# Column sums in four column groups, and a first stage in written order

## The chip, the cores and the metric

The kernel runs on one core of a Trainium2 chip, as a single launch. The metric is the device time of an execution in microseconds (us). The median of three runs before the change is 720.83 us (720.08 to 723.85).

PE is TensorE (matrix products into PSUM; PEld is its weight load), DVE is VectorE, ACT is ScalarE, POOL is GpSimd, and SP is the engine whose queue issues nearly all transfers.

## The reference, cut to what matters

One decoder block in fp32 with a sequence of 256 tokens, a model width D of 1024, and one conditioning row `c`:

```python
mod = silu(c) @ w_ada + b_ada                 # 1024 x 6144
sh1, sc1, g1, sh2, sc2, g2 = split(mod, 6)
h = rmsnorm(x, norm1_g) * (1 + sc1) + sh1
proj = h @ w_in                               # 1024 x 5120
# MoBA attention and differential attention from parts of proj,
# merged by sigmoid gates, projected by w_out
x = x + g1 * (merged @ w_out)
h2 = rmsnorm(x, norm2_g) * (1 + sc2) + sh2
x = x + g2 * moe(h2)                          # 32 experts, top 2 of one group
out = rmsnorm(x, final_g)
```

The change concerns `c @ w_ada` (the modulation, a product with a single row), the first `rmsnorm`, and the first products with `w_in`. The experts' weights, read later, are most of the bytes moved.

## The kernel before, in words

The stage that the change touches goes as follows. `x` is held as two tiles of 128 tokens. Each is squared and summed, the inverse root is taken by POOL's power (`rstd`, L335), the tile is scaled into `xn`, and sixteen transposes (L460) bring it into `xT`, with D on the partitions. `c` is transposed into `ccol` (L451), eight columns of 128.

For each quarter `q` of D (256 rows of `w_in`, so two chunks of 128) the modulation's `sc1` and `sh1` are needed for 256 columns. `ada_first(q)` (L376) makes them. In the first quarter both column blocks, later only `sh1`, are summed on PE (L387): the column `ccol[:, k]`, spread over 32 columns, is the stationary operand, and the product lands in partitions 32*(k % 4) and the 31 after it, so that four values of k share the array as four column groups. The block is evicted by ACT (L388). In the later quarters `sc1` is summed by DVE in eight operations (`ada_part`, L368 and L370). `ada_first_sum(q)` (L391) then turns the sums into columns with four small products (L397), which also add the four groups up, and three DVE operations (L399 to L401) make `modT`. `make_h` (L469) forms h (DVE, L471), its rounded part `xH` (ACT, L473) and the remainder `xL` (DVE, L474). `split` (L479) does the same to a weight chunk: ACT rounds it (L483), and DVE or POOL, in turn, subtracts (L486). `piece` (L489) then runs three products for each chunk and token tile (L496, L497, L498): `xH` by the rounded weights, `xL` by the rounded weights, `xH` by the remainder. In each of the four passes this is done for three blocks of 512 columns: k (into `acck`), q (`accq`) and v (`accv`). On PE the pass is written so:

```python
        piece(acck, chunks[0], xH, xL, 2 * q, q == 3)
        if q < 3:
            ada_first(q + 1)
        piece(accq, chunks[1], xH, xL, 2 * q, q == 3)
        if q < 3:
            ada_first_sum(q + 1)
            make_h(2 * q + 2)
        piece(accv, chunks[2], xH, xL, 2 * q, q == 3)
```

After the four passes come four small transposes (`p6`, L553), and the rest of the block follows. Between its further products stand eight units of the modulation: `ada_four(u)` (L403) sums 512 columns on PE (L409, again with four values of k as four column groups), ACT evicts them (L413), and `ada_sum(u)` (L415) turns them with four products (L430). In units 6 to 9 the columns of one product are taken with a step of four, in units 10 and 11 as whole blocks. Units 4 and 5 are turned in another way (L423).

Two things set the order of the work. Transfers are issued by SP in a list written out by hand (`order`), each as soon as its buffer is free. On the other engines the framework's scheduler orders the instructions, except inside `tc.manual_schedule(engines=...)`, where those engines keep the order of the program's text. SP is so ordered throughout, and from the first norm to `p6` so is PE (L447), but neither ACT nor DVE nor POOL.

Of the kernel before, what the change touches and what calls it, by code (L numbers as in the profile page):

```python
# [116 lines left out]
def tile_block(ctx: ExitStack, tc: tile.TileContext, d, out):  # L117
# [186 lines left out]

    io128 = cp.tile([128, 128], F32, name="io128")
# [3 lines left out]
    ident = cp.tile([128, 128], F32, name="ident")  # L309
    ve.tensor_scalar(ident, io128, pix, None, op0=OP.is_equal)  # L310
# [3 lines left out]
    ve.memset(nhalf, -0.5)  # L314
    th = cp.tile([128, 1], F32, name="th")
# [30 lines left out]
    gb1 = cp.tile([128, 2, KC], F32, name="gb1")  # L346
# [8 lines left out]
    def scale_base(i, g, b):  # L355
        ve.scalar_tensor_tensor(gb1[:, i, :], b, 1.0, g, op0=OP.add, op1=OP.mult)

# [5 lines left out]
    def ada_part(part, w, k0):  # L363

        for j in range(w.shape[1]):
            k = k0 + j
            if k == 0:
                ve.tensor_scalar(part, w[:, j, :], ccol[:, k:k + 1], None, op0=OP.mult)  # L368
            else:
                ve.scalar_tensor_tensor(part, w[:, j, :], ccol[:, k:k + 1], part, op0=OP.mult, op1=OP.add)  # L370

# [3 lines left out]

    def ada_first(q):  # L376

        p = wk(f"adc{q}")
        part = parts["first"] = turns["part"].new([2, 256])
        for i, n in enumerate((1, 0)):  # L380
            w = got[("adc", n, q)]
            o = p[:, 256 * i:256 * i + 256]
            if q and i == 0:
                ada_part(part[:, 0, :], w, 0)
            else:
                for k in range(KC):
                    te.matmul(o[32 * (k % 4):32 * (k % 4) + 32, :], c32(k), w[:, k, :], start=k < 4, stop=k >= 4)  # L387
                sc.activation(part[:, i, :], o, AF.Copy)  # L388
            done(("adc", n, q))

    def ada_first_sum(q):  # L391

        part, r = parts["first"], wk(f"adq{q}")
        k = slice(2 * q, 2 * q + 2)
        for i in range(2):
            for j in range(2):
                te.matmul(r[:, 2 * i + j:2 * i + j + 1], part[:, i, 128 * j:128 * j + 128],  # L397
                          ones[:, 0:1] if q and i == 0 else th, start=True, stop=True)
        ve.tensor_tensor(modT[:, 0, k], r[:, 0:2], vec[:, R_N1 + 2 * q:R_N1 + 2 * q + 2], op=OP.mult)  # L399
        ve.tensor_tensor(modT[:, 0, k], modT[:, 0, k], gb1[:, 0, k], op=OP.add)  # L400
        ve.tensor_tensor(modT[:, 1, k], r[:, 2:4], vec[:, R_B + 2 * q:R_B + 2 * q + 2], op=OP.add)  # L401

    def ada_four(u):  # L403

        p = wk(f"ada{u}")
        for h in range(2):
# [5 lines left out]
        parts[u] = turns["part"].new([512])  # L412
        sc.activation(parts[u], p, AF.Copy)  # L413

    def ada_sum(u):  # L415

        part = parts.pop(u)
        if u in (4, 5):
            q = wk(f"adaq{u}")
# [7 lines left out]
        q = wk(f"adaq{u}")  # L427
        for i in range(4):
            cols = slice(i, 512, 4) if seg in (3, 4) else slice(128 * i, 128 * i + 128)
            te.matmul(q[:, i:i + 1], part[:, cols], th, start=True, stop=True)  # L430
        if seg == 4:
            ve.tensor_tensor(modT[:, 2, k], q[:, 0:4], vecp[:, 0, k], op=OP.mult)
            ve.tensor_tensor(modT[:, 2, k], modT[:, 2, k], gb1[:, 1, k], op=OP.add)
# [12 lines left out]
    manual = ExitStack()  # L446
    manual.enter_context(tc.manual_schedule(engines={mybir.EngineType.PE}))  # L447
    ss1 = cp.tile([128, 2], F32, name="ss1")
    wps = wk("warm")
    warm(12, wps)  # L450
    sc.activation(ccol, columns(crow, KC, "crow"), AF.Silu)  # L451
    for t in range(2):
        ve.scalar_tensor_tensor(xn[:, t, :], x_sb[:, t, :], 1.0, x_sb[:, t, :], op0=OP.mult, op1=OP.mult,
                                accum_out=ss1[:, t:t + 1])
        rs1 = rstd(ss1[:, t:t + 1], D, f"rs1{t}")
        ve.tensor_scalar(xn[:, t, :], x_sb[:, t, :], rs1, None, op0=OP.mult)
# [9 lines left out]
    ve.tensor_copy(vec, columns(vrow, R_N, "vec_ps"))  # L466
    scale_base(0, vec[:, R_N1:R_N1 + 8], vec[:, R_B + 8:R_B + 16])

    def make_h(k0):  # L469
        for k in range(k0, k0 + 2):  # L470
            ve.tensor_scalar(hT[:, k, :], xT[:, k, :], modT[:, 0, k:k + 1], modT[:, 1, k:k + 1],  # L471
                             op0=OP.mult, op1=OP.add)
            sc.activation(xH[:, k, :], hT[:, k, :], AF.Copy)  # L473
            ve.tensor_sub(xL[:, k, :], hT[:, k, :], xH[:, k, :].bitcast(F32))  # L474
# [4 lines left out]
    def split(w, k0, n, name):  # L479
# [5 lines left out]
        nsplit[0] += 1  # L485
# [3 lines left out]
    def piece(acc, chunk, lh, ll, k0, last, ts=(0, 1)):  # L489
# [3 lines left out]
        for k in range(n):  # L493
# [36 lines left out]


    ada_first(0)
    ada_first_sum(0)
    acck, accq, accv = accs("ink"), accs("inq"), [wk(f"inv{t}") for t in range(2)]
    warm(4, acck[0])
    make_h(0)
    upto(("winq", 2, 3))
    for q in range(4):
        chunks = [split(got[("winq", u, q)], 0, 2, f"wq{u}{q}") for u in (1, 0, 2)]
        for u in (1, 0, 2):  # L540
# [9 lines left out]
        piece(accv, chunks[2], xH, xL, 2 * q, q == 3)  # L550
# [5 lines left out]
    scale_base(1, vecp[:, 0, :], vecp[:, 1, :])  # L556
# [714 lines left out]
```

## Time and profile before

| | |
|---|---|
| median of three runs | 720.83 us (720.08 to 723.85) |
| the profiled execution's own time | 719.79 us |
| its span, first to last instruction | 718.0 us |
| mean granted TensorE clock | 0.934 of full speed |
| busy: PE / DVE / ACT / POOL | 79% / 39% / 21% / 12% of the span |
| moved by DMA | 259.09 MB, 361 GB/s over the span |

The busy shares are means over stages that differ, so a stage has to be read by itself. A share of DMA of about 1 means that the transfer engines are busy all the time. A matmul's duration includes the way through the array, so that consecutive ones overlap: their pace is read from the chain of waits, which counts each only from the end of the one before.

### The profile page before, as it was taken

Reading aid. Unit: us, or ns where it says so; the run is one execution under the profiler, and the core shown is the slowest. Engines: PE = TensorE matmul, PEld = TensorE weight load, DVE = VectorE, ACT = ScalarE, POOL = GpSimd, SP = SyncE. Lnnn points to the kernel's source line nnn. Section 1 sums busy time; section 2 is a strip of 40 time slices with the busy share of each in tenths; the row PEclk is TensorE's granted clock in tenths of the full one; section 3 lists DMA queues with packets and bytes.
Section 4 is the critical chain, followed back from the end, with each engine's and each line's share of the span. In section 5 each row is a group of like instructions: output and inputs, shape, how many; then the busy total and the mean of one; then the engine's idle time right before and its main releaser. Section 6 shows DMA issues by size and latency. Waiting matters only on the chain.

```text
span 718.0 us, 11923 instructions
## 1 busy us (share of the span) xinstructions
PE 567.4 (79%) x4909; PEld 372.3 (52%) x4909; DVE 282.2 (39%) x806; ACT 147.8 (21%) x330; POOL 86.2 (12%) x73
## 2 busy tenths in 40 slices
PE   7989999999999998898886855965866685587374
PEld 3667666656777765564643522622623453264232
DVE  5778744545126647543432321321312121132105
ACT  2325664556444512000000000000000000000002
POOL 2225213315334310000000000000000000000001
PEclk9999999999999999899998988998998898899888
DMA  9999938909885798999999999999999999999992
GB/s 315 366 377 387 382 113 312 344 7 363 319 336 207 267 361 287 328 428 422 421 421 422 428 421 421 423 424 425 422 419 423 424 424 424 421 422 424 419 390 93
DMA packets 63582, 259.09 MB, mean 361 GB/s; under 512 B 6223, under 2 KB 16672, under 8 KB 45094
## 3 DMA queue, kind: packets, MB, share of 16 engines
q1 hardware_dynamic: 63430, 258.27, 91.4%
q8 instruction: 40, 0.66, 0.4%
q14 instruction: 16, 0.13, 0.0%
q10 hardware_dynamic: 96, 0.03, 0.0%
HBM read 257.23 MB, written 1.05 MB: 360 GB/s over the span
## 4 chain that ended last, share of the span: by engine, by line
DMA 51%; PE 33%; DVE 8%; issue 3%; ACT 2%; SPq 1%; POOL 1%; POOLq 0%; DVEq 0%; ACTq 0%
DMA gu<-in_w_up_dram 23%; DMA gu<-in_w_gate_dram 17%; DMA dn<-in_w_down_dram 10%; PE gu L979 3%; PE in L497 3%; PE in L496 3%; PE in L498 3%; PE xe L905 2%; PE dn L983 2%; PE ada L409 2%; DMA winq<-in_w_in_dram 1%; DVE part L370 1%; PE wo L496 1%; PE wo L497 1%; PE wo L498 1%
## 5 line engine op out<-in xcount | busy, mean ns | idle before, releaser
L979 PE MATMUL gu<-gu,xe 128*32 128x256 f32 x2048 | 137.4, 420 | 58.6 <-DMA gu<-in_w_up_dram 52.4
L979 PEld LDWEIGHTS gu<-gu,xe 128*32 128x32 f32 x2048 | 73.3, 118 | 117.5 <-issue 82.2
L983 PE MATMUL dn<-dn,hq 128*32 128x256 f32 x992 | 72.0, 439 | 59.2 <-DMA dn<-in_w_down_dram 42.2
L989 DVE TENSOR_TENSOR dq<-dn,g2g 32x256 f32<-32x256 f32 x124 | 52.1, 420 | 96.0 <-PE dn L983 92.5
L983 PEld LDWEIGHTS dn<-dn,hq 128*32 128x32 f32 x992 | 37.3, 123 | 93.3 <-issue 48.6
L970 ACT ACTIVATE hid<-gu 128x128 f32<-128x128 f32 x32 | 8.9, 278 | 347.1 <-PE gu L979 336.6
L971 DVE TENSOR_TENSOR hid<-hid,gu 128x128 f32<-128x128 f32 x32 | 9.2, 288 | 172.0 <-ACT hid L970 172.0
L905 PEld LDWEIGHTS xe<-pr,x 128*128 128x128 f32 x256 | 60.3, 329 | 4.2 <-issue 4.2
L905 PE MATMUL xe<-pr,x 128*128 128x128 f32 (+1 forms) x256 | 61.9, 403 | 0.0
L1074 POOL TENSOR_TENSOR fo<-fo,tail 128x512 f32<-128x512 f32 x2 | 2.5, 1272 | 442.3 <-ACT tail L1072 442.3
L486 POOL TENSOR_TENSOR win<-win,win 128x512 fp32r<-128x512 f32 x28 | 38.8, 1388 | 86.3 <-ACT win L483 79.4
L496 PE MATMUL in<-win,xH 128*128 128x512 f32 x112 | 45.7, 408 | 0.0
L497 PE MATMUL in<-win,xL 128*128 128x512 f32 x112 | 45.6, 407 | 0.0
L498 PE MATMUL in<-win,xH 128*128 128x512 f32 x112 | 45.2, 403 | 0.0
L483 ACT ACTIVATE win<-win 128x512 fp32r<-128x512 f32 x56 | 34.5, 629 | 20.4 <-PE in L498 19.7
L909 DVE TENSOR_SCALAR xe<-xe,modT 128x128 f32<-128x128 f32 (+1 forms) x64 | 21.6, 402 | 35.1 <-PE xe L905 35.1
L955 PE MATMUL y<-dq,pt 128*128 128x512 f32 x56 | 26.2, 610 | 5.9 <-DVE dq L989 5.8
L486 DVE TENSOR_TENSOR win<-win,win 128x512 fp32r<-128x512 f32 x28 | 22.7, 812 | 19.9 <-ACT win L483 17.8
L496 PEld LDWEIGHTS in<-win,xH 128*128 128x128 f32 x112 | 21.1, 188 | 7.8 <-issue 2.3
L497 PEld LDWEIGHTS in<-win,xL 128*128 128x128 f32 x112 | 21.2, 189 | 6.9 <-issue 3.2
L498 PEld LDWEIGHTS in<-win,xH 128*128 128x128 f32 x112 | 21.1, 188 | 6.7 <-issue 2.9
L955 PEld LDWEIGHTS y<-dq,pt 128*128 128x128 f32 x56 | 9.5, 189 | 20.2 <-DVE dq L989 13.5
(344 smaller groups left out, 755.2 us busy)
## 6 DMA issues: line engine op xcount, KB each, us to landing
gu<-in_w_gate_dram SPq DMA_DIRECT2D x54, 1024.0 KB, 22.9
gu<-in_w_up_dram SPq DMA_DIRECT2D x54, 1024.0 KB, 22.7
dn<-in_w_down_dram SPq DMA_DIRECT2D x26, 2048.0 KB, 24.7
ada<-in_w_ada_dram SPq DMA_DIRECT2D x16, 1024.0 KB, 10.8
win<-in_w_in_dram SPq DMA_DIRECT2D x14, 1024.0 KB, 11.6
gu<-in_w_gate_dram SPq DMA_DIRECT2D x20, 512.0 KB
gu<-in_w_up_dram SPq DMA_DIRECT2D x20, 512.0 KB, 7.0
dn<-in_w_down_dram SPq DMA_DIRECT2D x10, 1024.0 KB, 8.2
```

Of the source, the lines that this page charges most:

```text
L409: te.matmul(p[32 * j:32 * j + 32, :], c32(4 * h + j), w[:, j, :], start=h == 0, stop=h == 1)
L483: sc.activation(wh, w[:, k0:k0 + n, :], AF.Copy)
L486: eng.tensor_sub(wl, w[:, k0:k0 + n, :], wh.bitcast(F32))
L496: te.matmul(acc[t], lh[:, k0 + k, s], wh[:, k, :], start=k0 + k == 0, stop=False)
L497: te.matmul(acc[t], ll[:, k0 + k, s], wh[:, k, :], start=False, stop=False)
L498: te.matmul(acc[t], lh[:, k0 + k, s], wl[:, k, :], start=False, stop=last and k == n - 1)
L905: te.matmul(p[:, w * i:w * i + w], x_sb[:, t, 512 * g + i:512 * g + 512:4], self.pr[:, t, s], start=t == 0, stop=t == 1)
L909: ve.tensor_scalar(self.xe[:, k, s], p[:, w * i:w * i + w], modT[:, 2, k:k + 1], modT[:, 3, k:k + 1], op0=OP.mult, op1=OP.add)
L955: te.matmul(y[:, t, 512 * n:512 * n + 512], self.pt[rows, 128 * t:128 * t + 128], self.dq[rows, 512 * n:512 * n + 512], start=False, stop= ...
L979: te.matmul(gu[32 * j:32 * j + 32, 0:256], xe, w[:, :, 128 * j:128 * j + 128], start=first, stop=last)
L983: te.matmul(dn[32 * j:32 * j + 32, 0:256], hq[:, 32 * k:32 * k + 32], w[:, 256 * j:256 * j + 256], start=k == 0, stop=k == 3)
L989: ve.tensor_tensor(dq[s, 256 * j:256 * j + 256], dn[r, 0:256], g2g[0][r, :], op=OP.mult)
```

## The change

- Constants are reordered, and hand-written order begins already there, now for PE, DVE, ACT and POOL; it ends, as before, after `p6`.
- Sums: the four column groups now hold four blocks of columns, all eight values of k summed in PSUM, where before they held four values of k. In the first quarter the groups are 64 columns wide, one column block of 256 after the other; in the later quarters 128 wide, both blocks interleaved, and DVE's sums go. In units 6 to 11 the groups are 128 wide, with a step of four in units 6 to 9. Units 4 and 5 stay.
- Turning: one product with four columns of the identity (`one4`) in place of four products, in the later quarters and in units 6 to 11; in the first quarter four smaller ones. Two DVE operations instead of three make `modT` from a prepared block `ab`.
- Norm: tile 0 is squared by DVE, tile 1 by ACT; one `rstd` for both; tile 0 is scaled by DVE, tile 1 by ACT. POOL runs one power early. The bias columns are transposed ahead of `x` and copied between the two tiles.
- Passes: the two-chunk splits are all on DVE. Each block's weights are split where its products are written. The sums of the next quarter stand after the q block, the turning and `make_h` in the middle of the v block. In the first pass the k block's products with the remainder come last.

```diff
+    manual = ExitStack()
+    manual.enter_context(tc.manual_schedule(engines={mybir.EngineType.PE, mybir.EngineType.DVE,
+                                                     mybir.EngineType.Activation, mybir.EngineType.Pool}))
...
+    one4 = ident[:, 0:128:32]
+
+    def sums(o, w, k, cols):
+
+        for g, c in enumerate(cols):
+            te.matmul(o[32 * g:32 * g + 32, :], c32(k), w[:, c], start=k == 0, stop=k == KC - 1)
+
     def ada_first(q):
 
         p = wk(f"adc{q}")
...
+        part = parts["first"] = turns["part"].new([128])
+        w = [got[("adc", n, q)] for n in (1, 0)]
+        if q:
+            for k in range(KC):
+                for i in range(2):
+                    for j in range(2):
+                        g = 32 * (2 * i + j)
+                        te.matmul(p[g:g + 32, 0:128], c32(k), w[i][:, k, 128 * j:128 * j + 128],
+                                  start=k == 0, stop=k == KC - 1)
+            sc.activation(part, p[:, 0:128], AF.Copy)
+        else:
+
+            for i in range(2):
+                o = p[:, 64 * i:64 * i + 64]
                 for k in range(KC):
-                    te.matmul(o[32 * (k % 4):32 * (k % 4) + 32, :], c32(k), w[:, k, :], start=k < 4, stop=k >= 4)
-                sc.activation(part[:, i, :], o, AF.Copy)
+                    sums(o, w[i][:, k, :], k, [slice(64 * g, 64 * g + 64) for g in range(4)])
+                sc.activation(part[:, 64 * i:64 * i + 64], o, AF.Copy)
+        for n in (1, 0):
             done(("adc", n, q))
...
+        if q:
+            te.matmul(r[:, 0:4], part, one4, start=True, stop=True)
...
+        ve.tensor_tensor(modT[:, 0:2, k], v3(r[:, 0:4], 2), ab[:, 0, :, k], op=OP.mult)
+        ve.tensor_tensor(modT[:, 0:2, k], modT[:, 0:2, k], ab[:, 1, :, k], op=OP.add)
...
             for j in range(4):
-                te.matmul(p[32 * j:32 * j + 32, :], c32(4 * h + j), w[:, j, :], start=h == 0, stop=h == 1)
+                if u in (4, 5):
+                    te.matmul(p[32 * j:32 * j + 32, :], c32(4 * h + j), w[:, j, :], start=h == 0, stop=h == 1)
+                else:
+                    sums(p[:, 0:128], w[:, j, :], 4 * h + j, [slice(g, 512, 4) if u // 2 in (3, 4) else
+                                                             slice(128 * g, 128 * g + 128) for g in range(4)])
...
-            te.matmul(q[:, i:i + 1], part[:, cols], th, start=True, stop=True)
+        te.matmul(q[:, 0:4], part, one4, start=True, stop=True)
...
-    warm(12, wps)
+    warm(4, wps)
     sc.activation(ccol, columns(crow, KC, "crow"), AF.Silu)
+    warm(8, wps)
+    ve.scalar_tensor_tensor(xn[:, 0, :], x_sb[:, 0, :], 1.0, x_sb[:, 0, :], op0=OP.mult, op1=OP.mult,
+                            accum_out=ss1[:, 0:1])
+    sc.activation(xn[:, 1, :], x_sb[:, 1, :], AF.Square, accum_out=ss1[:, 1:2])
+    rs1 = rstd(ss1, D, "rs1")
+    ve.tensor_scalar(xn[:, 0, :], x_sb[:, 0, :], rs1[:, 0:1], None, op0=OP.mult)
+    sc.activation(xn[:, 1, :], x_sb[:, 1, :], AF.Copy, scale=rs1[:, 1:2])
+    vec_ps = columns(vrow, R_N, "vec_ps")
...
         eng = gp if nsplit[0] % 2 else ve
-        nsplit[0] += 1
+        nsplit[0] += n == 1
...
+        def chunk(u):
+            c = split(got[("winq", u, q)], 0, 2, f"wq{u}{q}")
             done(("winq", u, q))
-        feed()
-        piece(acck, chunks[0], xH, xL, 2 * q, q == 3)
+            feed()
+            return c
+
+        c = chunk(1)
+        if q:
+            piece(acck, c, xH, xL, k0, last)
+        else:
+
+            for l, w in ((xH, c[0]), (xL, c[0]), (xH, c[1])):
+                for k in range(2):
+                    for t in range(2):
+                        te.matmul(acck[t], l[:, k, 128 * t:128 * t + 128], w[:, k, :],
+                                  start=k == 0 and l is xH and w is c[0], stop=False)
+        piece(accq, chunk(0), xH, xL, k0, last)
         if q < 3:
             ada_first(q + 1)
-        piece(accq, chunks[1], xH, xL, 2 * q, q == 3)
+        c = chunk(2)
+        piece(accv, c, xH, xL, k0, False, ks=(0,))
         if q < 3:
             ada_first_sum(q + 1)
             make_h(2 * q + 2)
-        piece(accv, chunks[2], xH, xL, 2 * q, q == 3)
+        piece(accv, c, xH, xL, k0, last, ks=(1,))
```

## Rows read from the trace of the kernel before

**Rows 1.** The page: DMA's busy tenths in 40 equal slices of the span

```profile
DMA  9999938909885798999999999999999999999992
```

**Rows 2.** Table of stretches: us, busy by engine (instructions), granted clock, DMA share, GB/s

```profile
66.00:80.00 14.00, 14.00 (x76) 10.61 (x76) 11.50 (x36) 9.21 (x22) 1.87 (x3) 1.00 1.05 387
...
150.00:160.00 10.00, 9.58 (x46) 5.60 (x47) 4.93 (x19) 4.80 (x13) 1.29 (x1) 1.00 0.01 2
...
190.00:200.00 10.00, 10.00 (x57) 7.01 (x56) 1.60 (x4) 5.01 (x9) 3.88 (x3) 1.00 0.74 247
...
400.00:700.00 300.00, 198.66 (x2203) 115.51 (x2199) 66.62 (x183) 9.71 (x28) 0.00 (x0) 0.89 1.01 421
```

**Rows 3.** Chain of waits, first stage: start us, us, engine, tile, line

```profile
17.45 1.26 DVE modT L400
...
19.65 0.80 PE ink L496
...
24.16 1.00 PE adc L387 x16
...
28.11 0.80 PE adq L397 x8
...
41.63 1.02 PE adq L397 x8
...
45.20 0.43 PE inv L497
...
65.72 0.23 PE inv L497
...
66.17 0.57 PE p L553 x4
```

**Rows 4.** Timelines of single engines: start us, us, instruction, idle before it

```profile
13.52 1.05 ACT L483 ACTIVATE wq<-winq 128x1024 fp32r<-128x1024 f32 x1
14.47 0.38 ACT L388 ACTIVATE part<-adc 128x256 f32<-128x256 f32 x1
...
43.53 0.74 ACT L473 ACTIVATE xH<-hT 128x256 fp32r<-128x256 f32 x2 [5.54 <-DVE hT L471]
...
33.81 7.67 DVE L370 SCALAR_TENSOR_TENSOR part<-adc,ccol,part 128x256 f32<-128x256 f32 x7
...
42.88 0.16 DVE L400 TENSOR_TENSOR modT<-modT,gb 128x2 f32<-128x2 f32 x1
43.08 0.73 DVE L471 TENSOR_SCALAR hT<-xT,modT 128x256 f32<-128x256 f32 x2
...
52.32 1.23 DVE L486 TENSOR_TENSOR wq<-winq,wq 128x1024 fp32r<-128x1024 f32 x1 [3.67 <-ACT wq L483]
...
38.07 2.61 POOL L486 TENSOR_TENSOR wq<-winq,wq 128x1024 fp32r<-128x1024 f32 x1 [0.39 <-ACT wq L483]
...
9.60 3.39 PE L460 MATMUL xt<-ident,xn 128*128 128x128 f32 x16 [1.70 <-DVE xn L456]
...
704.86 0.65 PE L1046 MATMUL dn<-dn,hq 128*32 128x64 f32 x32
```

**Rows 5.** Table of stretches again, one us of the third pass

```profile
44.00:45.00 1.00, 1.00 (x4) 0.72 (x3) 1.00 (x3) 0.27 (x1) 0.00 (x0) 0.50 1.04 383
```

**Rows 6.** Single lines: duration ns min/median/max, first and last start us, form

```profile
L1046 PE MATMUL dn<-dn,hq x128: 219/219/243, 701.9 to 706.9; 128*32 128x64 f32 x128
...
L979 PE MATMUL gu<-gu,xe x64: 376/379/403, 273.3 to 276.6; 128*32 128x256 f32 x64
...
L920 PE MATMUL xr<-x,pr x16: 617/632/636, 269.3 to 270.7; 128*32 128x256 f32 x16
...
L388 ACT ACTIVATE part<-adc x5: 367/385/387, 14.5 to 50.9; 128x256 f32<-128x256 f32 x5
```

**Rows 7.** Chain of waits, later sums and their turning

```profile
127.22 1.85 PE ada L409 x16
...
130.20 1.63 PE adaq L430 x8
...
195.13 0.79 PE adaq L430 x8
```

More of the change, by code (lines that the diff above doesn't have):

```diff
@@ L314, in tile_block @@
     ve.memset(nhalf, -0.5)
+    ident = cp.tile([128, 128], F32, name="ident")
+    ve.tensor_scalar(ident, io128, pix, None, op0=OP.is_equal)
     th = cp.tile([128, 1], F32, name="th")
@@ L393, in ada_first_sum @@
         part, r = parts["first"], wk(f"adq{q}")
-        k = slice(2 * q, 2 * q + 2)
[L395 to L401, printed above, removed]
+        if q:
+            te.matmul(r[:, 0:4], part, one4, start=True, stop=True)
+        else:
+            for i in range(2):
+                for j in range(2):
+                    te.matmul(r[64 * j:64 * j + 64, 2 * i:2 * i + 2], part[:, 64 * i:64 * i + 64], one4[:, j::2],
+                              start=True, stop=True)
+        k = slice(2 * q, 2 * q + 2)
+        ve.tensor_tensor(modT[:, 0:2, k], v3(r[:, 0:4], 2), ab[:, 0, :, k], op=OP.mult)
+        ve.tensor_tensor(modT[:, 0:2, k], modT[:, 0:2, k], ab[:, 1, :, k], op=OP.add)
     def ada_four(u):
         p = wk(f"ada{u}")
+        n = 512 if u in (4, 5) else 128
         for h in range(2):
@@ L426, in ada_sum @@
         seg, k = u // 2, slice(4 * (u % 2), 4 * (u % 2) + 4)
-        q = wk(f"adaq{u}")
-        for i in range(4):
-            cols = slice(i, 512, 4) if seg in (3, 4) else slice(128 * i, 128 * i + 128)
-            te.matmul(q[:, i:i + 1], part[:, cols], th, start=True, stop=True)
+        te.matmul(q[:, 0:4], part, one4, start=True, stop=True)
         if seg == 4:
             ve.tensor_tensor(modT[:, 2, k], q[:, 0:4], vecp[:, 0, k], op=OP.mult)
-            ve.tensor_tensor(modT[:, 2, k], modT[:, 2, k], gb1[:, 1, k], op=OP.add)
+            ve.tensor_tensor(modT[:, 2, k], modT[:, 2, k], gb1[:, k], op=OP.add)
         elif seg == 3:
@@ L465, in tile_block @@
                 ve.tensor_copy(o, v3(p, 4))
-    ve.tensor_copy(vec, columns(vrow, R_N, "vec_ps"))
-    scale_base(0, vec[:, R_N1:R_N1 + 8], vec[:, R_B + 8:R_B + 16])
+        if t == 0:
+            ve.tensor_copy(vec, vec_ps)
+            ve.tensor_copy(ab[:, 0, 0], vec[:, R_N1:R_N1 + 8])
+            ve.memset(ab[:, 0, 1], 1.0)
+            ve.scalar_tensor_tensor(ab[:, 1, 0], vec[:, R_B + 8:R_B + 16], 1.0, vec[:, R_N1:R_N1 + 8],
+                                    op0=OP.add, op1=OP.mult)
+            ve.tensor_copy(ab[:, 1, 1], vec[:, R_B:R_B + 8])
     def make_h(k0):
-        for k in range(k0, k0 + 2):
+        ks = range(k0, k0 + 2)
+        for k in ks:
             ve.tensor_scalar(hT[:, k, :], xT[:, k, :], modT[:, 0, k:k + 1], modT[:, 1, k:k + 1],
@@ L473, in make_h @@
             sc.activation(xH[:, k, :], hT[:, k, :], AF.Copy)
+        for k in ks:
             ve.tensor_sub(xL[:, k, :], hT[:, k, :], xH[:, k, :].bitcast(F32))
@@ L484, in split, with piece @@
         eng = gp if nsplit[0] % 2 else ve
-        nsplit[0] += 1
+        nsplit[0] += n == 1
         eng.tensor_sub(wl, w[:, k0:k0 + n, :], wh.bitcast(F32))
         return wh, wl
-    def piece(acc, chunk, lh, ll, k0, last, ts=(0, 1)):
+    def piece(acc, chunk, lh, ll, k0, last, ts=(0, 1), ks=None):
         wh, wl = chunk
         n = wh.shape[1]
-        for k in range(n):
+        for k in range(n) if ks is None else ks:
             for t in ts:
@@ L532, in tile_block @@
     ada_first(0)
+    acck, accq, accv = accs("ink"), accs("inq"), [wk(f"inv{t}") for t in range(2)]
+    warm(2, acck[0])
     ada_first_sum(0)
-    acck, accq, accv = accs("ink"), accs("inq"), [wk(f"inv{t}") for t in range(2)]
-    warm(4, acck[0])
+    warm(3, acck[0])
     make_h(0)
@@ L538, in tile_block @@
     for q in range(4):
-        chunks = [split(got[("winq", u, q)], 0, 2, f"wq{u}{q}") for u in (1, 0, 2)]
-        for u in (1, 0, 2):
+        k0, last = 2 * q, q == 3
+        def chunk(u):
+            c = split(got[("winq", u, q)], 0, 2, f"wq{u}{q}")
             done(("winq", u, q))
-        feed()
-        piece(acck, chunks[0], xH, xL, 2 * q, q == 3)
+            feed()
[3 more added lines that the diff above has]
+            piece(acck, c, xH, xL, k0, last)
+        else:
+            for l, w in ((xH, c[0]), (xL, c[0]), (xH, c[1])):
[4 more added lines that the diff above has]
+        piece(accq, chunk(0), xH, xL, k0, last)
         if q < 3:
             ada_first(q + 1)
-        piece(accq, chunks[1], xH, xL, 2 * q, q == 3)
+        c = chunk(2)
+        piece(accv, c, xH, xL, k0, False, ks=(0,))
         if q < 3:
```

36 lines of the change are left out of this document (7 added, 29 removed).

## The prediction, made before the result was known

> **What bounds the kernel now.** I read the page's slices first: the DMA engines are busy through most of the span, but between roughly a quarter and a half of it their share falls away, once to nearly nothing [rows 1]. The table of stretches says why. From 150 to 160 us PE is busy 9.58 of 10 us while the DMA share is 0.01, and PE is as full at 66 to 80 and 190 to 200; from 400 us on it is the other way round, DMA 1.01 and PE 198.66 of 300 [rows 2]. So the kernel has two halves: up to some 280 us PE sets the pace and the queue waits for buffers that PE's work gives back, after that the weights stream without a gap. A microsecond that PE loses in the first half moves the start of the stream and comes out at the end in full; I carry it at 1:1. Up to 90 us the queue has work whatever PE does, so the first products do not lack data: their last weights were asked for long before.
>
> The change lies in two places, so I read the chain of waits there. The stage of the first products runs from its first product at 19.65 to the four small transposes at 66.17: **46.5 us** [rows 3]. A product of 512 columns costs 0.23 us at full clock and 0.43 at half [rows 3]. 144 of them are 32.8 us (0.228 each); the three later column sums cost 1.00 and their turning 0.80 each, 5.4 us; together 38.2. The other 8.3 us are waits and slow clock. The largest is in the third pass: DVE's sums take 7.67 us, stretched by POOL's splits at the same time, and PE does not reach the turning before 41.63 [rows 4, 3]; then products take 0.43 us at a granted clock of 0.50, which is 1.2 GHz [rows 3, 5]. Each such slow stretch (that at the start too) costs about 1.8 us: nine products at 0.2 us more.
>
> **The change in the stage of first products.** *Removed:* DVE's sums (24 instructions) and POOL's share of the splits, so the collision and its 3.3 us of PE idleness go. *Added on PE:* each later pass sums both column blocks, 32 products of 128 columns, 64 instructions, where 16 of 256 columns took 1.00 us [rows 3]. In four column groups, instructions of 64, 256 and 512 columns go through at a rate that follows the columns (a 64-column one lasts 219 ns, a 256-column one 379, that is 0.83 ns a column over a fixed part [rows 6]), so four times the instructions at a quarter of the columns cost what one block did before, twice: about 1.85 us (1.7 to 2.05). The turning shrinks from eight instructions to two: 0.25 instead of 0.80. PE work per pass becomes 8.2 + 1.85 + 0.25 = 10.3 us, against 10.0.
>
> *Moved, and this decides:* today only PE is in written order. ACT is not: it split weights at 13.52 before it evicted a sum at 14.47, though the text has the eviction first [rows 4]. After the change ACT and DVE follow the text, and the text puts four waits into each pass:
> 1. The sums stand after the second product block, and ACT's split for the third block stands behind the eviction of the sums. When PE has ended the sums, ACT evicts (256 columns took 385 ns [rows 6]; 128, say, 0.27), then splits (1.05 us [rows 4]); PE has nothing else in its order: 1.35 us.
> 2. The third product of that block needs DVE's half of the split, 1.23 us [rows 4], of which the two products before it cover 0.46: 0.8 us.
> 3. After the turning: two small DVE operations (0.16 us each [rows 4], 0.4 with their gaps), the first h (0.42), two roundings on ACT (0.43 and 0.35; the pairs are 0.73 and 0.74 [rows 4]), and only behind these ACT's split for the next pass, 1.05. That is 2.65 us; PE has six products (1.37) for it: 1.3 us.
> 4. DVE's half of that split again: 0.8 us. The first pass is spared this one by its own order of products.
>
> What is queued behind ACT's waiting eviction is exactly the split that PE wants next, so nothing hides it. Sum: first pass 10.3 + 3.45 = 13.75; second and third 10.3 + 4.25 = 14.55 each; last 8.2 + 0.8 = 9.0; together 51.9 us at full clock.
>
> *The start.* The norm's halves run on two engines, which puts the transposes a little ahead of 9.60; they took 3.39 us [rows 4]. The first sums become 128 instructions of 64 columns (0.65 us for 32 of them with the tail [rows 4], some 13.5 ns each: 1.7 us, 3.4 at half clock). With evictions and turning I put the end of the turning at 14.5 to 18, middle 16.2. Today a small DVE operation stands there for 1.26 us [rows 3], beside a POOL split; that goes, but the weight split now stands behind the roundings: 2.7 us from turning to first product. That gives 18.9 (17.2 to 20.7), so 0.75 earlier than today's 19.65.
>
> End of the stage: 18.9 + 51.9 = 70.8 against 66.17, **+4.6 us** at full clock (+1 to +7).
>
> *Clock.* Today's 46.5 us hold two slow stretches; 51.9 holds none. PE stands still at the start as it does now, so I count one of them, 1.8 us; none is the lower end. Pairs of waits within 3 us in each pass could cost one each: up to 7 us. **+1.8.**
>
> **The change in the later sums.** Six units (of eight) go to four groups. Today one costs 1.85 us for the sum and 1.63 for the turning where columns are taken with a step of four (four units), 0.79 where not (two) [rows 7]. The turning becomes two instructions with whole weights, about 0.25: 4 x 1.38 + 2 x 0.54 = 6.6 us gained. The sum streams as many columns, but in the four units the moving operand now steps by four elements. The trace has one such product: 256 columns with a step of four last 632 ns, 256 whole ones 379 [rows 6]. Over the fixed part (166 ns) that is 466 against 213, a factor of 2.19. Sixteen batches of four then take 16 x 0.233 = 3.7 us instead of 1.7: 4 x 2.0 = 8.1 us lost. PE is full there [rows 2]. Net **+1.5 us** (lower end -0.5, if the row overstates the step; upper +3).
>
> Here the row and a page meet. The Trainium skill, SBUF — State Buffer, section "Door 1: The DMA port swizzle", says that SBUF is read in 16-byte lines, that an access crossing to a new line pays, and it counts a step of four fp32 elements as the reach that is still free. Read as a penalty for every new line it agrees with the 632 ns; read as "four is free", the measurement differs and decides. By that second reading the sum would be 728.7 - 8.1 = 720.6.
>
> The edits to constants, to the bias block (five small DVE copies beside PE's transposes) and the early power on POOL cost nothing: they lie before x has been normalised or beside PE's work; uncovered they are under 1 us.
>
> **Sum.** 4.6 + 1.8 + 1.5 = 7.9 us on this execution's 719.79 us (span 718.0 and 1.8 around it): 727.7. The median of the runs shown is 1.04 above this execution, so I predict **728.7 us**.
>
> **Rivals.**
> *Faster: the waits do not come.* If ACT's splits are there in time, because the framework lets them pass the eviction or because PE's sums end earlier than I think, the removed collision is what remains. For: the collision and two slow stretches are real and go away. Against: PE, in its hand-ordered stretch, runs sums and products strictly as written [rows 3], and the same keyword now names ACT and DVE. With all 12.8 us of waits (3.45 + 2 x 4.25 + 0.8) and the slow stretch gone: 728.7 - 12.8 - 1.8 = 714.1. It decides if the waits come to less than 12.8 - 7.9 = 4.9 us, about 1.6 in each of the first three passes. Chance 0.17.
> *Step of four is free.* The 632 ns could hold something else, since that product waits for DVE between its halves. Then 8.1 us go: 720.6, no change. For: that wait; the Trainium skill's wording, above, would allow it. Against: the duration is that of each instruction, the first ones too. Chance 0.12.
> *The clock falls in every pass.* Three more stretches of 1.8 us: 734. For: after 3.3 us of idleness it did fall; against: no single wait here is over 1.4 us. Chance 0.10.
> *As summed:* 0.61.
>
> From these: slower by over 0.5% (3.6 us, about what a measurement of this kernel tells from no change) 0.71, within 0.5% 0.12, faster 0.17. As summed the range is 723 to 734; the 8-in-10 range must reach into the faster case: 715 to 735.
>
> **What would show it.** In the changed profile: first product near 19 us and the small transposes near 71 to 73 us; in each of the first three passes PE idle before the third block, released by ACT's split, and again before the next pass's first block; DVE's accumulations gone, no POOL work before the last pass; the turning at 0.2 to 0.3 us; sums of the four stepped units near 3.8 us, of the other two near 1.9. The prediction is wrong if ACT splits ahead of the eviction, if stepped sums stay at 1.9 us, or if the chain from 70 to 280 us is released by DMA.

## The result, and the profile after

The changed kernel takes **733.22 us** (median of 4 runs, 729.27 to 736.67) against 720.54 before: a ratio of 1.0156, 95% interval 1.0115 to 1.0197. It is slower, inside the predicted range and 4.5 us above the predicted time. The profiled execution is the slowest of its four (736.67 us, span 734.8), so its sum is made against the profiled one of before (719.79): 16.9 us, where the forecast added up 7.9. By the medians it is 12.7.

Where they come from is read off PE's timeline at marks that both kernels have. The four small transposes that end the stage of the first products start at 66.10 us before and 78.67 after (the chain of waits says 66.17 and 78.74): +12.57. The first expert product starts at 273.31 and 288.39: +15.08, so another 2.5 us are lost between. From there to the end 444.7 and 446.4 us pass: +1.7, in a part where the weights stream; in the profiled executions of all kernels below this part lies between 443.8 and 446.8.

The chain of waits of the changed kernel, first stage (start us, us, engine, tile, line), answers to [rows 3]:

```profile
19.89 3.02 PE ink L580 x12
...
25.63 1.93 PE adc L388 x64
...
27.58 0.28 ACT part L390
27.86 0.95 ACT wq L507
...
28.83 1.24 DVE wq L510
...
31.31 0.13 PE adq L405 x2
...
78.74 0.57 PE p L593 x4
```

The sums cost 1.93 us and their turning 0.13, as forecast. Between them the chain leaves PE: eviction of the sums, split on ACT, split on DVE. PE's own timeline shows what that costs in every pass (start us, us, instruction, and in brackets PE's idle time before it and what ended it):

```profile
28.85 0.50 PE L520 MATMUL inv<-wq,xH 128*128 128x512 f32 x1 [1.34 <-ACT wq L507]
...
30.11 0.50 PE L522 MATMUL inv<-wq,xH 128*128 128x512 f32 x1 [0.53 <-DVE wq L510]
...
34.05 0.50 PE L520 MATMUL ink<-wq,xH 128*128 128x512 f32 x1 [1.15 <-ACT wq L507]
...
35.31 0.79 PE L522 MATMUL ink<-wq,xH 128*128 128x512 f32 x1 [0.53 <-DVE wq L510]
...
67.88 0.50 PE L520 MATMUL ink<-wq,xH 128*128 128x512 f32 x1 [1.63 <-ACT wq L507]
...
69.14 0.55 PE L522 MATMUL ink<-wq,xH 128*128 128x512 f32 x1 [0.52 <-DVE wq L510]
```

These are the four waits of the prediction, in its order, and they come in all three passes. ACT's timeline answers to [rows 4]: the eviction now stands ahead of the split, and ACT has been idle for 6.79 us when it comes.

```profile
27.58 0.28 ACT L390 ACTIVATE part<-adc 128x128 f32<-128x128 f32 x1 [6.79 <-PE adc L388]
27.75 1.05 ACT L507 ACTIVATE wq<-winq 128x1024 fp32r<-128x1024 f32 x1
```

The table of stretches (us, busy by engine, granted clock, DMA share, GB/s) answers to [rows 5]. It is cut so that each row holds one fall of the clock:

```profile
34.00:40.00 6.00, 5.42 (x16) 4.05 (x17) 2.36 (x2) 0.95 (x2) 0.00 (x0) 0.72 1.10 352
50.00:57.00 7.00, 5.75 (x17) 4.29 (x18) 2.55 (x3) 1.62 (x2) 0.00 (x0) 0.76 1.05 386
67.00:74.00 7.00, 5.59 (x16) 4.16 (x17) 6.49 (x7) 4.81 (x7) 3.16 (x2) 0.76 1.05 388
```

A stretch of 6 us at 0.72 has lost 6 x 0.28 = 1.7 us; so have the others. After each second pair of waits TensorE runs on at 1.2 GHz for 3.4 us: three falls, 5.0 us. At the start of the stage, where the prediction had counted one, the clock stays at 1.00; here the slow stretch lay ahead of the first product:

```profile
8.00:15.00 7.00, 5.54 (x80) 4.97 (x80) 3.08 (x11) 2.35 (x3) 0.00 (x0) 0.51 1.08 363
```

That is 7 x 0.49 = 3.4 us lost ahead of it. The kernel before lost 1.7 there (0.76 over the same 7 us) and 1.7 behind its first product (0.66 from 19 to 24).

The later sums (one line's durations in ns, min/median/max) answer to [rows 6]: 128 whole columns last 272 ns, 128 with a step of four 405. By the chain of waits a unit lasts 3.74 us stepped and 1.88 whole (in the timeline, with the way through the array, 3.81 and 1.95); turning is two instructions in 0.2 us.

```profile
L376 PE MATMUL ada<-ada,ccol x384: 272/405/407, 139.1 to 223.4; 128*32 128x128 f32 x192
```

One place was not in the forecast. Behind the norm of the second attention PE waits 2.37 us, then runs at half clock (0.76 from 183 to 190 us, 1.7 us lost); before, the same transposes waited 0.67 and the clock stayed. PE's timeline, before and after:

```profile
171.05 0.30 PE L724 MATMUL odt<-ident,ods 128*128 128x128 f32 x1 [0.67 <-DVE ods L721]
```

```profile
183.95 0.76 PE L764 MATMUL odt<-ident,ods 128*128 128x128 f32 x3 [2.37 <-DVE ods L761]
```

From there to the next unit's sum 6.3 us passed before and 9.5 now. Of these 3.2 us, 1.7 are the half clock; the rest is work that has moved: 29 products with `win` instead of 23 now stand between these marks. DVE's timeline shows what is late, again before and after, and POOL's what runs at the time:

```profile
168.90 0.17 DVE L340 TENSOR_TENSOR rsdu<-rsdu,rsdm 128x8 f32<-128x8 f32 x1
```

```profile
180.73 2.29 DVE L344 TENSOR_TENSOR rsdu<-rsdu,rsdm 128x8 f32<-128x8 f32 x1
183.05 0.17 DVE L345 TENSOR_SCALAR rsdu<-rsdu 128x8 f32<-128x8 f32 x1
```

```profile
180.63 2.36 POOL L780 TENSOR_TENSOR oml<-omf,omh 128x1024 fp32r<-128x1024 f32 x1
```

An operation on 8 elements a partition lasts 2.29 us where its neighbour lasts 0.17. POOL's split of the first attention's output (`oml`) runs from 180.63 for 2.36 us, exactly beside it; in the kernel before it came at 170.45, after that operation.

### The profile page after: what moved, and what is told of

It is laid out like the page before. It is cut to its first block, busy times and chain, and to the rows that moved or that the text cites. A ratio compares the mean times of both kernels' runs of the same rounds, so it can differ in the third digit from the quotient of the medians.

```text
span 734.8 us, 12846 instructions
## 1 busy us (share of the span) xinstructions
PE 578.7 (79%) x5384; PEld 380.6 (52%) x5384; DVE 271.8 (37%) x781; ACT 147.3 (20%) x333; POOL 69.6 (9%) x67
## 4 chain that ended last, share of the span: by engine, by line
DMA 53%; PE 33%; DVE 8%; ACT 3%; issue 1%; POOL 1%; SPq 0%; POOLq 0%; DVEq 0%; ACTq 0%
DMA gu<-in_w_up_dram 22%; DMA gu<-in_w_gate_dram 18%; DMA dn<-in_w_down_dram 10%; PE in L520 3%; PE in L522 3%; PE in L521 2%; PE gu L1019 2%; PE ada L376 2%; PE xe L945 2%; DMA win<-in_w_in_dram 2%; PE dn L1023 1%; ACT p L677 1%; PE wo L520 1%; PE wo L521 1%; PE wo L522 1%
## 5 line engine op out<-in xcount | busy, mean ns | idle before, releaser
L1019 PE MATMUL gu<-gu,xe 128*32 128x256 f32 x2048 | 140.4, 425 | 56.8 <-DMA gu<-in_w_up_dram 49.2
L1023 PE MATMUL dn<-dn,hq 128*32 128x256 f32 x992 | 76.0, 458 | 56.8 <-DMA dn<-in_w_down_dram 38.4
L522 PE MATMUL in<-win,xH 128*128 128x512 f32 x112 | 46.6, 416 | 0.0
L520 PE MATMUL in<-win,xH 128*128 128x512 f32 x112 | 45.8, 409 | 0.0
L510 DVE TENSOR_TENSOR wq<-winq,wq 128x1024 fp32r<-128x1024 f32 x12 | 14.3, 1222 | 26.8 <-ACT wq L507 26.8
```

The source lines that it names most:

```text
L510: eng.tensor_sub(wl, w[:, k0:k0 + n, :], wh.bitcast(F32))
L520: te.matmul(acc[t], lh[:, k0 + k, s], wh[:, k, :], start=k0 + k == 0, stop=False)
L522: te.matmul(acc[t], lh[:, k0 + k, s], wl[:, k, :], start=False, stop=last and k == n - 1)
L1019: te.matmul(gu[32 * j:32 * j + 32, 0:256], xe, w[:, :, 128 * j:128 * j + 128], start=first, stop=last)
L1023: te.matmul(dn[32 * j:32 * j + 32, 0:256], hq[:, 32 * k:32 * k + 32], w[:, 256 * j:256 * j + 256], start=k == 0, stop=k == 3)
```

## The experiments

Marks from PE's timelines, in us: the first product, the small transposes, the first expert product; then the median and the ratio to the kernel before with its interval. The kernel before was timed again beside each group of runs, with medians from 720.5 to 722.0, so kernels of different groups are better compared by their ratios. The marks are of one execution each, and a fall of the clock between two of them counts in.

| kernel | first product | transposes | expert | median | ratio |
|---|---|---|---|---|---|
| before | 19.65 | 66.10 | 273.31 | 720.54 | 1 |
| changed | 19.89 | 78.67 | 288.39 | 733.22 | 1.0156 (1.0115 to 1.0197) |
| third split first | 20.16 | 68.45 | 278.21 | 726.64 | 1.0066 (1.0045 to 1.0088) |
| order on PE only | 20.77 | 66.09 | 276.94 | 724.79 | 1.0038 (1.0015 to 1.0060) |
| all splits early | 19.94 | 60.69 | 272.28 | 720.31 | 0.9990 (0.9972 to 1.0008) |
| waits filled | 19.39 | 75.05 | 287.45 | 732.74 | 1.0148 (1.0117 to 1.0179) |
| old stepped units | 18.89 | 79.32 | 286.21 | 732.28 | 1.0140 (1.0112 to 1.0167) |
| early + old stepped | 18.94 | 61.28 | 268.32 | 716.94 | 0.9933 (0.9911 to 0.9956) |
| early + late `oml` | 19.11 | 61.45 | 269.27 | 717.03 | 0.9938 (0.9915 to 0.9961) |
| early + old + late `oml` | 19.14 | 59.93 | 266.95 | 716.17 | 0.9925 (0.9903 to 0.9947) |
| whole columns | 19.00 | 61.32 | 265.85 | 712.57 | 0.9856 (0.9818 to 0.9893) |
| permuted eviction | 18.96 | 59.72 | 265.67 | 713.17 | 0.9873 (0.9838 to 0.9907) |
| first rounding early | 18.97 | 59.82 | 264.01 | 711.55 | 0.9848 (0.9814 to 0.9883) |

**Is it the order on ACT?** One line is moved:

```
+        c = chunk(2)
         if q < 3:
             ada_first(q + 1)
-        c = chunk(2)
```

> The changed kernel with the third block's weight split written before the column sums instead of behind their eviction. Theory (the time went into waits that the written order of ACT and DVE makes): the first pair of waits, 1.34 and 0.53 us in each of the first three passes, goes, 5.6 us in all: 727.6 us against 733.2; if the three slow-clock stretches of 1.87 us go with them, 722. The second pair (1.15 and 0.53) stays. Rival (PE would have waited there anyway, on data or on the sums): no change, 733.

The first pair of waits is gone, the second has stayed, and two of the three falls went too: the stage ends 10.2 us earlier, the median is 6.6 us lower. PE's timeline has only these left in a pass (the first of three is shown; the one fall came in the third):

```profile
32.12 0.50 PE L520 MATMUL ink<-wq,xH 128*128 128x512 f32 x1 [1.13 <-ACT wq L507]
...
33.38 0.50 PE L522 MATMUL ink<-wq,xH 128*128 128x512 f32 x1 [0.53 <-DVE wq L510]
```

The rival, that PE would have waited there anyway, falls: PE had work, and the data was there.

**Is it written order as such?** Only PE keeps it:

```
-    manual.enter_context(tc.manual_schedule(engines={mybir.EngineType.PE, mybir.EngineType.DVE,
-                                                     mybir.EngineType.Activation, mybir.EngineType.Pool}))
+    manual.enter_context(tc.manual_schedule(engines={mybir.EngineType.PE}))
```

> The changed kernel with only PE in written order, ACT, DVE and POOL placed by the framework as before; products and sums as changed. Theory (the written order on ACT and DVE is the cost, not the new sums): the framework puts both splits ahead of the eviction and of the roundings, all four waits go (3 x 1.87 + 2 x 1.68 + 0.5, some 9.5 to 11 us) and the slow-clock stretches with them (5.6 us): 717 to 720 us, the first stage near 43 us instead of 58.9. Rival (the new sums and their turning themselves are the cost): 730 to 733, the stage still above 55 us.

The framework does put both splits ahead of the eviction and of the roundings, and no split is waited for. But the gain is smaller than expected: the stage ends where it ended before the change, 66.09, with a later start (20.77) and other waits in the place of the old ones, now for the rounded h and its low half:

```profile
32.16 0.49 PE L519 MATMUL ink<-wq,xH 128*128 128x512 f32 x1 [0.59 <-ACT xH L495]
...
33.51 0.50 PE L520 MATMUL ink<-wq,xL 128*128 128x512 f32 x1 [0.85 <-DVE xL L497]
```

So the new sums are not dear, and most of the loss was the order; taking DVE's sums away does not by itself end the stage earlier (it lasts 45.3 us against 46.5, from a start 1.1 later).

**An order without the waits.** The splits are taken apart into rounding and subtraction:

```
+        c = chunk(2)
         if q < 3:
             ada_first(q + 1)
...
+            early = rounded(got[("winq", 1, q + 1)], 0, 2, ...)
             ada_first_sum(q + 1)
             make_h(2 * q + 2)
...
-        if q:
-            piece(acck, c, xH, xL, k0, last)
-        else:
+        for i, (l, w) in enumerate(((xH, c[0]), (xL, c[0]), (xH, c[1]))):
```

> All engines in written order as changed, but the order written otherwise: the third block's split before the sums, the next pass's first rounding on ACT before h is rounded, and each pass takes its products as high x high, low x high, high x low, so that the low half of the weights is wanted last. Theory (waits of the order plus the clock they drop): all four waits and the three slow-clock stretches go, 9.5 to 11 plus 5.6 us: 717 to 720 us. If the waits go but the clock falls all the same: 723. Rival (written order on all engines costs by itself, whatever the order): above 728.

The stage's waits and falls are gone, and PE is busy through all of it, which the table of stretches shows:

```profile
20.00:40.00 20.00, 20.00 (x199) 15.94 (x200) 8.82 (x12) 7.11 (x10) 0.00 (x0) 1.00 1.08 364
40.00:60.00 20.00, 20.00 (x143) 15.67 (x143) 14.22 (x21) 9.74 (x16) 4.53 (x3) 1.00 1.05 386
```

The stage ends at 60.69, 18.0 us before the changed kernel's and 5.4 before the old one's, with the same products, sums and turnings on PE: 40.75 us instead of 58.78. The whole run, though, is no faster than before. The 5.4 us are given back later: 1.0 before the first softmax, 0.9 up to the norm's transposes and 3.2 from them to the next unit's sum (the pause of 2.37, the half clock and the moved products are there as in the changed kernel), 0.6 in small steps; the two whole units add 1.35. At the first expert product 1.0 is left.

**Pauses or load?** The waits are kept and filled with products nobody reads:

```
             sc.activation(part, p[:, 0:128], AF.Copy)
+            parts["r"] = wk(f"adq{q}")
+            warm(5, parts["r"])
...
+                if fill and k == t == 0:
+                    warm(2, fill)
                 te.matmul(acc[t], lh[:, k0 + k, s], wl[:, k, :], ...)
...
         piece(accv, c, xH, xL, k0, last, ks=(1,))
+        if q < 3:
+            warm(4, parts["r"])
```

> The changed kernel with its four waits per pass kept, but filled with idle products of constants (5, 2, 4 and 2 products of 512 columns, 0.23 us each), whose results nobody reads. Theory (the three slow-clock stretches of 1.87 us come from the pauses of PE): the granted clock stays at 2.4 GHz through the stage, 5.6 us go: 727.6 us. Rival (the clock falls for another reason, the load itself): the stretches of 0.50 stay, 733 or more.

In the stage the theory holds: the three stretches that fell are at 1.00, and the transposes start 3.6 us earlier. (The fall at 20 us is the one of the start: this execution lost 1.7 us ahead of the first product, where the changed kernel's lost 3.4.) The time does not follow. From 153 to 160 us the granted clock is 0.51, where the changed kernel has the same softmax pauses and no fall:

```profile
20.00:24.00 4.00, 4.00 (x12) 3.14 (x11) 1.73 (x2) 0.29 (x1) 0.00 (x0) 0.57 1.06 382
34.00:40.00 6.00, 5.68 (x25) 3.57 (x23) 3.00 (x4) 2.06 (x3) 0.00 (x0) 1.00 1.09 352
50.00:57.00 7.00, 6.69 (x38) 4.74 (x42) 2.36 (x2) 1.13 (x2) 0.00 (x0) 1.00 1.05 386
67.00:74.00 7.00, 6.92 (x31) 5.73 (x31) 7.00 (x9) 2.76 (x5) 3.35 (x2) 1.00 1.05 386
153.00:160.00 7.00, 7.00 (x21) 5.27 (x21) 3.06 (x15) 2.60 (x9) 0.27 (x1) 0.51 0.00 0
```

That is 7 x 0.49 = 3.4 us back. Filled pauses did keep the clock up where they were filled; that this is worth time in the end is not shown by this run, and why the clock fell at 153 us is open.

**The stepped sums.** In the changed kernel the four stepped units go back:

```
-        n = 512 if u in (4, 5) else 128
+        n = 512 if u < 10 else 128
...
+        if u < 10:
+            for i in range(4):
+                te.matmul(q[:, i:i + 1], part[:, i::4], th, ...)
```

> The changed kernel with the four stepped units of the later sums back as before (four values of k in four groups of 512 whole columns, turned with four products whose weights are stepped); the other two units stay new. Theory (stepped sums last 3.74 us instead of 1.85, turning 0.2 instead of 1.63, and PE then stands 2.37 us before the transposes behind the differential norm and runs on at half clock, 3.2 us in all): 4 x 1.89 less, 4 x 1.43 more and the 3.2 back, 733.2 - 1.8 - 3.2 = 728.2 us. Rival 1 (only the arithmetic of sums and turnings, the stop has another cause): 731.4. Rival 2 (a step of four costs nothing, the old turning only costs): 738.9.

From the transposes to the first expert product it is 2.8 us faster (206.9 against 209.7), but the medians can't be told apart. PE's pause before the norm's transposes is back at 0.66, yet the clock fell after it all the same (0.76 over 7 us, 1.7 lost), as it does not in the same program below. The same edit on top of the early splits:

> The kernel with all splits early, and the four stepped units back as before. Theory (the first stage is worth -5.4 us by itself, and the stepped units with the stop at the norm lose it again): 720.3 - 3.2 - 0.3 to 2.0 = 715 to 717 us, faster than the kernel before. Rival (the later loss has nothing to do with the units): 720.

Here it comes out: 0.9933 against 0.9990, 4.1 us, and faster than the kernel before. The stop at the norm is gone with the edit, and 6.3 us pass again to the next unit.

**What makes the stop.** `oml` is held back by a constant that DVE writes after the next unit's sum:

```
+        if u == 7:
+            one = small.tile([128, 1], F32, tag="one", name="one")
+            ve.tensor_scalar(one, modT[:, 3, 7:8], 0.0, 1.0, op0=OP.mult, op1=OP.add)
...
-    sc.activation(omh, omf, AF.Copy)
+    sc.activation(omh, omf, AF.Copy, scale=one)
```

> The kernel with all splits early and the new stepped units, but the split of the first attention's output (ACT 1.1 us, POOL 2.4 us) held back by one small DVE operation until the next unit's sum, so that it no longer runs beside the differential norm's small DVE operations, one of which lasted 2.28 us instead of 0.17. Theory (that collision makes the stop): the transposes of the norm come 1.1 to 2.1 us earlier, and if PE's pause gets short enough the half clock goes too: 717 to 719.2 us. Rival (the stop comes from PE having too little other work there, or from another collision): 720, the small operation short and the pause still above 2 us.

DVE's and PE's timelines:

```profile
165.32 0.17 DVE L344 TENSOR_TENSOR rsdu<-rsdu,rsdm 128x8 f32<-128x8 f32 x1
```

```profile
166.43 0.30 PE L767 MATMUL odt<-ident,ods 128*128 128x128 f32 x1 [0.35 <-DVE ods L764]
```

2.28 us became 0.17, the pause 0.35, and the clock stayed. From the first sum of the pair ahead of the norm to the next unit's sum the early splits alone take 24.2 us and this kernel 20.5: of the 3.7 us, 2.0 are the pause and 1.7 the clock. The median is 3.3 us lower. With the stepped sums kept, this gains as much as undoing them.

The same chain holds more of this, which no run moved: the operation before that one (it too has two inputs, one tile twice) lasts 1.22 to 1.24 us in every kernel here, this one included, beside POOL's split of a `win` chunk (1.28 us); and with the old stepped units another, two operations on, lasts about 1.2 and not 0.17. Both together:

> The kernel with all splits early, the four stepped units as before, and the split of the first attention's output held back. Theory: PE has work enough with the old units that the norm's chain is nearly covered; the 0.67 us pause that the kernel before has there goes at most: 715 to 716.5 us. Rival: the split costs more where it is put, 717 or more.

716.17, within the intervals of the two: they mend one stop. Of the net cost of the four stepped units 0.8 us are left between the marks (207.8 against 207.0).

**What the step would be worth.** Against the early splits with late `oml` one slice differs: `slice(128 * g, 128 * g + 128)` in the place of `slice(g, 512, 4)`. It leaves out the columns' right places, so it measures the step and is no kernel to use.

> All splits early, the first attention's split held back, and the four units' new sums read whole columns instead of a step of four. Left out: the columns' right places, so the second norm's modulation takes wrong values; the work is the same but for the step. Theory 1 (a step of four costs PE 1.86 us a unit, and PE sets the pace everywhere): 717.0 - 4 x 1.86 = 709.6 us. Theory 2 (two of the four units stand ahead of the differential norm's transposes, where the norm's chain sets the pace and not PE): only the other two count, 713.3, and PE's pause before the transposes grows from 0.35 to some 4 us. Rival (the step is no cost to the time): 717.

4.5 us less by the medians, 5.9 by the ratios, 3.3 between the marks. The two units that stand alone gave 1.85 and 1.87 (from the start of their sums to the next fixed mark 2.67 instead of 4.52, 13.22 instead of 15.09); the two ahead of the norm gave 2.3 of their 3.7, and the pause grew from 0.35 to 2.19. In this execution 2.7 us were lost ahead of them, where the granted clock from 130 to 154 us was 0.86; without that loss the marks give 6.0. So the result lies between the two theories (7.4 and 3.7 us): the units that stand alone gave all, and the pair ahead of the norm some three fifths and not nothing. Each product of the sums lasts what a whole one should:

```profile
L376 PE MATMUL ada<-ada,ccol x384: 272/273/297, 123.6 to 200.8; 128*32 128x128 f32 x192
```

**Keeping the order of columns without a step on PE.** The old sums, evicted in order:

```
+            sc.activation(parts[u].rearrange("p (i c) -> p i c", i=4), p.rearrange("p (c i) -> p i c", i=4), AF.Copy)
...
-                te.matmul(q[:, i:i + 1], part[:, i::4], th, ...)
+                te.matmul(q[:, i:i + 1], part[:, 128 * i:128 * i + 128], th, ...)
```

> All splits early, the first attention's split held back, the four stepped units summed and turned as before, but ACT evicts their sums with the columns put in order, so that the four turning products take whole weights (0.79 us instead of 1.63). Theory: 716.2 - 4 x 0.84 = 712.8 us if PE sets the pace everywhere, 714.5 if the two units ahead of the norm's transposes gain nothing there. Rival (ACT's permuted eviction gets longer than 0.60 us by as much as PE gains): 716.

The groups by line show ACT's four evictions at the 598 ns that whole ones take:

```profile
L433 ACT ACTIVATE part<-ada 128x512 f32<-128x512 f32 x4 | 2.4, 598 | 3.0 <-PE ada L423 3.0
...
L431 ACT ACTIVATE part<-ada 128x512 f32<-128x512 f32 x2 | 1.2, 598 | 2.5 <-PE ada L423 2.5
```

713.17, 3.0 us less than with the old sums and late `oml` (3.8 by the ratios); the units that stand alone gave 0.85 each, the pair ahead of the norm 0.87 of its 1.7, while the pause there grew from 0.65 to 1.50. After it the clock fell in this execution (1.7 us between 164 and 168); after the same pause in the next kernel's it did not. Last, the pause ahead of the stage's first product, 1.87 us in all kernels with early splits:

```
+    early = rounded(got[("winq", 1, 0)], 0, 2, "wq10")
     ada_first(0)
```

> As the one with the permuted eviction, and the first pass's first rounding of weights too is put ahead, on ACT before the eviction of the first sums, where ACT stands idle. Theory: the first product of the stage comes 1.0 us earlier (19.1 to 18.1), and the pause of 1.87 us ahead of it, after which the clock fell in some executions, becomes 0.9: 1.0 to 2.4 us less than the one with the permuted eviction. Rival (the weights have not landed by then, or the eviction of the sums is pushed back by the rounding): no gain, or a loss of up to 1 us.

The pause is 0.60 as meant, but this execution came to it late: its first sums begin at 13.37 us instead of 12.17, ahead of all that the edit moves. So the first product stands at 18.97, as without it. Between 8 and 16 us this execution lost 3.4 us to the clock, the one without the edit 1.7; from the first sums to the first product it takes 5.6 us, where 6.7 to 6.9 pass in the other kernels whose first sums ran slow:

```profile
18.97 1.20 PE L589 MATMUL ink<-wq,xH 128*128 128x512 f32 x4 [0.60 <-ACT xH L503]
```

The median, 711.55, is 1.6 us lower than without the edit; the intervals of the two overlap. It has the lowest median here, not told apart from the two above it, and it is faster than the kernel before: 0.9848.

## Why the prediction was right, and where it was off

*The stage's work.* Sums 1.93 (forecast 1.85) and turning 0.13 (0.25) came as worked out. DVE's sums left the stage, and POOL's splits of its weights too; POOL's first split, of the next stage's `win`, comes at 63.24 us, in the third pass.

*The four waits.* All came, released by the instructions named: 1.34, 0.53, 1.15, 0.53 idle in the first round (forecast 1.35, 0.8, 1.3, 0.8). At full clock the passes last 14.2, 15.0, 15.5 and 9.2 us (16.67, 17.16 and 10.86, less 1.7 each, after the first) against 13.75, 14.55, 14.55 and 9.0: 1.9 more. This excess is not in the waits as a whole. The same work without waits and falls takes 40.75 us (all splits early), so the waits cost 58.8 - 5.0 - 40.75 = 13.0 us, and 12.8 were forecast; the work itself was summed at 39.1, 1.7 too low. The sums and their turning came as forecast; where PE goes from products to sums or back, two starts lie 0.32 to 0.34 us apart and not 0.23, which makes part of it. That the order of ACT and DVE makes the waits, and that PE waits for nothing else there, is shown by the two kernels that write the splits earlier.

*The start.* 19.89 instead of 18.9: 1.0 more. It goes with the longer slow stretch ahead of it. Old stepped units, whose program is the same up to there, lost 1.7 us and not 3.4 between 8 and 15 us; its first product came at 18.89, and its clock then fell at 19, as the prediction had it.

*The clock: the term that was mis-sized.* The prediction took one fall, at the start, 1.8 us, and gave "the clock falls in every pass" 0.10, since no single wait was over 1.4 us. There were three in the passes, 5.0 us, and the one of the start lay ahead of the first product. The end of the stage was forecast at 18.9 + 51.9 + 1.8 = 72.6 and came at 78.74: 1.0 + 1.9 + 3.2 more. What that rival said is what happened, and its price, 734, is nearer to the measured 733.2 than the sum is. With both pairs of waits in a pass the clock fell in all three passes of both such executions (changed, old stepped units); with the second pair alone in one of three; with the waits filled in none. So the time lay inside the range because the range had room for this, not because the sum had it.

*The later sums.* The net of +1.5 came out at +2.5 up to the experts, but of other parts. Steps cost what the row gave (3.74 against a forecast of 3.7; by the second reading of the Trainium skill's sentence, in the prediction, it would have been 1.9), the two whole units gained 1.35 together (from the first of their sums to the first product of the second projection, `wpd`, 22.25 us before, 20.90 after; forecast 1.1). What is missing is the stop at the norm: 1.7 us more pause and 1.7 us of half clock. The sentence that failed is that PE is full there, so that the sum alone decides (its rows end at 160 us and go on at 190, beside the place and not on it): ahead of the norm's transposes the chain through ACT, POOL and DVE ends last, so what turning gained there could be had only in part, and a POOL operation that the framework now set beside a small DVE one made that chain longer. Without the stop the net of the four stepped units is some 0.8 us, below the 2.6 that they had in the sum.

*1:1.* A microsecond at the end of the first stage comes out at the end only where nothing between takes it back: the early splits gained 5.4 us and 1.0 arrived at the experts; with the old stepped units the stop at the norm went, and of 4.8 gained in the stage 5.0 arrived, of 6.2 (with the late `oml`) 6.4.

*The rivals.* "The waits do not come", made true by the early splits, gave 720.3 and not 714.1: its price left out the stop (717.0 without it), and with it the work that was summed 1.7 us too low; it also took the fall at the start for gone, and that one stayed, before the first product or behind it, in most executions. "The step is free" is refuted by the durations and by the run with whole columns.

*A row read loosely.* DMA's share falls away from the sixth to the sixteenth of the 40 slices, so from an eighth to two fifths of the span and not "between roughly a quarter and a half". No term of the sum hangs on it.

## What to carry to other kernels

When an engine is put in written order, read its text as a queue: what stands behind an instruction that waits for PE is what PE may want next; write the work whose inputs have long landed ahead of it, and use the part that comes last (here the low halves) last. Price short waits in pairs with the clock that they can drop, and do it for each repetition. And before counting PE time as gained, look in each place for the chain that ends last: beside a short DVE chain, a long POOL operation can cost more than what was saved.

## What the runs showed of the hardware beyond that

- The clock does not follow the length of the pause alone. The same 1.87 us ahead of the first product, in the same order of instructions, was followed by 1.2 GHz in some executions (early + old stepped: its first twelve products take 4.4 us) and not in others (early + old + late `oml`: 2.9 us). After a pause of 0.66 us ahead of the norm's transposes it fell once and once not, after 1.50 once and once not, after 2.19 it did not. From the stage's first product up to the experts most falls cost 1.7 us; two cost 3.4, with the waits filled and with whole columns, each behind a pause of 0.69 that every kernel has in the softmax. Executions of one kernel lie up to some 4 us from their median (one 5.8), which is one to three falls; why the clock falls in one and not in the other stays open.
- A DVE operation with two inputs of 8 elements took 2.28 us beside a POOL subtraction and 0.17 without it. The Trainium skill, SBUF — State Buffer, section "Who interferes with whom", says that a DVE instruction with two SBUF inputs contends with a GpSimd instruction that reads SBUF; the trace agrees, to the length of the whole POOL operation (2.36 us).
- ACT reads 512 PSUM values with a step of four in 598 ns, as fast as whole ones; PE's moving operand from SBUF with the same step took 405 ns instead of 272 for 128 columns.
